# Strassen combinations of h in a stream of their own, in a hybrid decoder block

## The chip, the core and the metric

The kernel runs on one core of one Trainium2 chip. It is one launch, written in Bass with the Tile framework. The metric is the time of the launch on the device in microseconds (us). The five engines are TensorE (PE), VectorE (DVE), ScalarE (ACT), GpSimd (POOL) and SyncE (SP). SP issues every DMA of this kernel. Each engine works through its own instructions in the order in which they were placed when the program was built.

## The reference

For x of shape (1, 2048, 1024) in float32 the layer computes:

```
mod = c @ w_ada + b_ada -> shift/scale/gate for the mixer and for the FFN
h = rms_norm(x, g_pre_mix) * (1 + scale_m) + shift_m
proj = h @ w_in -> attn q (512) k (128) v (128), mLSTM q k v o (512 each), i f (8), gates A B (1024 each)
branch A: rotary q, k; sliding window (128) GQA with sinks, 8 query and 2 key heads of 64
branch B: causal conv4 + SiLU on mLSTM q, k; chunkwise stabilised mLSTM; head norm; sigmoid(o)
x = x + gate_m * rms_norm((sigmoid(gA) * (A @ w_a) + sigmoid(gB) * (B @ w_b)) @ w_out, g_post_mix)
h2 = modulate(rms_norm(x, g_pre_ffn)); ff = (silu(h2 @ w_gate) * (h2 @ w_up)) @ w_down
x = x + gate_f * rms_norm(ff, g_post_ffn)
```

The products are made in near full float32 precision: each operand is split into a rounded part `hi` and the rest `lo`, and a product is three matmuls, hi·hi + hi·lo + lo·hi (`mm3`).

## The kernel before

**Tiling.** The 2048 tokens are four blocks of 512, and two blocks make a superblock (`superblock(sb)`, with blocks `b0` and `b1`). h of a block is kept transposed, features on the 128 partitions, as eight 128x512 tiles, four per half of the features.

**One superblock.** In this order PE does: attention q and k|v of b0 (`q_kv(b0)`), mLSTM v of b0 (`vm(b0)`), then k|v, q and v of b1, and then fourteen pairs of feature tiles (mLSTM q, k, o and the gates) for both blocks at once. The fourteen pairs use Strassen's scheme (`pair_parts`): seven products instead of eight. Its right operands are the quarters of h, named 11, 21, 12 and 22 (half of the features, then block), and four combinations of them, T1 to T4. Then come the outputs of b0 and of b1. The FFN follows after both superblocks.

**How h of the second block is made.** `hprep(b1)` loads x (two tiles of 256 rows), takes the squares on ACT, scales the rows on DVE, and waits. Then `one(k)` makes one feature tile: four PE transposes into a PSUM tile of the pool `mix`, two ACT passes of 128x512 out of it (L518 writes the rounded hi, L520 writes the plain value v), and a DVE subtraction (L521) for lo. For the second block of a superblock the v of all four quarters are kept in the tiles `HR["T1"]` to `HR["T4"]`. After `one(k)` and `one(k + 4)`, four DVE subtractions of 128x512 (L534 to L537) turn the four v tiles of index k into the combinations T1 to T4, in place.

**How T2 and T4 become operands.** `hsums(("T2", "T4"))` issues two DMAs (L545) that copy the combinations from SBUF to SBUF, 1 MB each, into new buffers, and then makes hi on ACT (L551) and lo on DVE (L552), eight times each. It is spawned when the keys of b1 are about to start. `hsums(("T1", "T3"))` follows when v of b1 is done, since its buffers come from quarter 12 of h.

**What sets the order.** The program is written by `run2` and by streams. `run2` goes through the parts of the projections: it issues the next weight load, splits the weights of the parts ahead (L256 and L257 for q, L259 and L260 for the rest: hi on ACT, lo on DVE), and writes the matmuls of a part. Every matmul adds its planned cost to the planner's clock `now`. After every three matmuls `tick()` lets each stream whose due time has come write its next step; a stream yields how long it wants to wait by that clock, in ns. `finish` moves the clock until a stream is done. Streams are `hprep`, `hsums`, the rotary and transposing of q and k (`q_stream`, `k_stream`), the mLSTM gates (`gates`: DVE work on the pre-gates, PE transposes, scans on DVE, two small DMAs, PE transposes again), and two attention streams that each take every second 128-token block. The Tile framework (`schedule_with_timeline_sim=True`) then places each instruction in the queue of its engine: it follows the order written, but takes another instruction where the first is not ready by the time line that it works out. So the queues are fixed when the program is built.

**Attention.** For a 128-token block `attention(n)` loads q, k and v from a DRAM buffer (`at`, two buffers in SBUF), writes 24 score matmuls into four `mix` banks, copies and masks them (ACT L931, DVE L933), takes the maxima (DVE L938 to L941), 8 exponentials on ACT (L946), the sums on DVE (L948, L949), the division on POOL (L950), transposes of the probabilities on PE, and the product with v. The keys come from `k_stream`: rotary on DVE (L757 to L761), a PE transpose, ACT L797 and DVE L798, and DMA stores (L801).

**Pools.** `mix` and `acc` are four PSUM banks each, `tx` nine SBUF tiles (the evacuated q, k, v and the scratch of the rotary), `big` fourteen SBUF tiles of 1 MB (x, h, the combinations), and split weights four tiles.

Of the kernel before, what the change touches and what calls it, by code (L numbers as in the profile page):

```python
# [28 lines left out]
T2 = 1024  # L29
# [6 lines left out]
NEG = -1.0e30  # L36


L_X, L_HT, L_HS = 16000.0, 1400.0, 1500.0
L_ROPE, L_ROPEK, L_QK, L_ATT2 = 5000.0, 2100.0, 1500.0, 3500.0  # L40
L_GATE, L_SCAN = 1800.0, 3000.0
L_SOFT, L_PT, L_PV = 8000.0, 1300.0, 1000.0
# [29 lines left out]
def decoder_block(ctx: ExitStack, tc: tile.TileContext, a: dict, out: bass.AP, dbg=None):  # L72
# [20 lines left out]
    def nm(s):  # L93
        uid[0] += 1
        return f"{s}{uid[0]}"
# [4 lines left out]
    def mix_tile():  # L100
        return ps_mix.tile([P, 512], F32, tag="mix", name=nm("mix"))
# [7 lines left out]
    def big(shape, dtype=F32):  # L109
        t = bpool.tile([P, 2048], dtype, tag="big", name=nm("big"))  # L110
        return t.rearrange("p (k c) -> p k c", k=shape[0])
# [4 lines left out]
    def load_x(src, big, i):  # L116
        xb = big([2, D])
        nc.sync.dma_start(xb, src[i * 256:(i + 1) * 256, :].rearrange("(t p) c -> p t c", p=P))
        return xb
# [86 lines left out]
    def transpose(o, i):  # L206
        now[0] += 110.0
        k = i.shape[0]
        T.transpose(o, i, ident[:k, :k])  # L209

    def spawn(gen, delay=0.0):
        st = [now[0] + delay, gen, False]
        streams.append(st)
        return st
# [15 lines left out]
    def finish(sts):  # L230
        for st in sts:
            while not st[2]:
                now[0] = max(now[0], min(q[0] for q in streams))
                tick()
# [235 lines left out]
    def rsqrt_of_sumsq(ss, n, eps=EPS):  # L470

        ms = small.tile([P, 4], F32, tag="ms", name=nm("ms"), bufs=4)
        V.tensor_scalar(ms[:, :n], ss, 1.0 / D, eps, op0=ALU.mult, op1=ALU.add)  # L473
        r = small.tile([P, 4], F32, tag="rs", name=nm("rs"), bufs=6)
        G.tensor_tensor(r[:, :n], ms[:, :n], nhalf[:, :n], op=ALU.pow)  # L475
        return r
# [3 lines left out]
    def hc_part(name, i):  # L480
        st = HC.setdefault(name, [None, None])
        if st[i] is None:
            st[i] = big([4, TB], F32R)
        return st[i]

    def hprep(b, first=False):

        odd = b % 2
        xs = []
        xbs = x_first if first else [load_x(x_d[b * TB:(b + 1) * TB, :], big, i) for i in range(2)]  # L490
        V_NAMES = ("T3", "T2") if odd else ("T1", "T4")
        for n in V_NAMES:
            HR[n] = big([4, TB])
        vs = [HR[n] for n in V_NAMES]
        for i in range(2):
            xb = xbs[i]
            ss = small.tile([P, 4], F32, tag="ss", name=nm("ss"), bufs=4)
            for t in range(2):
                for hf in range(2):
                    A.activation(vs[i][:, 2 * t + hf, :], xb[:, t, hf * 512:(hf + 1) * 512], AF.Square,  # L500
                                 accum_out=ss[:, 2 * hf + t:2 * hf + t + 1])
            V.tensor_tensor(ss[:, 0:2], ss[:, 0:2], ss[:, 2:4], op=ALU.add)
            r = rsqrt_of_sumsq(ss[:, 0:2], 2)
            for t in range(2):
                if first:
                    A.activation(xb[:, t, :], xb[:, t, :], AF.Copy, scale=r[:, t:t + 1])
                else:
                    V.tensor_scalar(xb[:, t, :], xb[:, t, :], r[:, t:t + 1], None, op0=ALU.mult)
                xs.append(xb[:, t, :])
        yield L_X  # L510

        def one(k):
            name = f"{k // 4 + 1}{odd + 1}"
            hi, lo = (hc_part(name, i)[:, k % 4, :] for i in range(2))
            ps = mix_tile()
            for t in range(NT):
                transpose(ps[:, t * P:(t + 1) * P], xs[t][:, k * P:(k + 1) * P])
            A.activation(hi, ps, AF.Identity, scale=s1[:, k:k + 1], bias=sh1[:, k:k + 1])  # L518
            v = vs[k // 4][:, k % 4, :]
            A.activation(v, ps, AF.Identity, scale=s1[:, k:k + 1], bias=sh1[:, k:k + 1])  # L520
            (G if first else V).tensor_tensor(lo, v, hi.bitcast(F32), op=ALU.subtract)  # L521

        if not odd:
            for k in range(KD):
                one(k)
                yield L_HT
            return
        for k in range(4):
            one(k)
            yield L_HT  # L530
            one(k + 4)
            yield L_HT
            t1, t2, t3, t4 = (HR[n][:, k, :] for n in ("T1", "T2", "T3", "T4"))
            V.tensor_tensor(t1, t3, t1, op=ALU.subtract)  # L534
            V.tensor_tensor(t3, t2, t3, op=ALU.subtract)
            V.tensor_tensor(t2, t2, t1, op=ALU.subtract)
            V.tensor_tensor(t4, t4, t2, op=ALU.subtract)  # L537
            yield L_HT

    def hsums(names):  # L540

        for name in names:
            raw = HR.pop(name)
            lo = hc_part(name, 1)
            nc.sync.dma_start(lo.bitcast(F32), raw)  # L545
        yield L_HD
        for name in names:
            hi, lo = (hc_part(name, i) for i in range(2))
            for k in range(4):
                v = lo[:, k, :].bitcast(F32)  # L550
                A.copy(hi[:, k, :], v)  # L551
                V.tensor_tensor(lo[:, k, :], v, hi[:, k, :].bitcast(F32), op=ALU.subtract)  # L552
                yield L_HS
# [157 lines left out]
    def c_tile(n):  # L711
        C[n] = kvp.tile([P, MH, MD + 1], F32, tag="cst", name=nm("cst"), bufs=3)
        return C[n]

    hp0 = hprep(0, first=True)
    next(hp0)
    tables = {}
# [18 lines left out]
    def superblock(sb):  # L736
# [83 lines left out]
        def q_kv(b):  # L820
            raw_kv = Raw(load_kv)
            return token_group(srcs_rows(w_in, KD, C_Q), KD, 512, lhs_h(b), evac_q(b), pair_heads=True), token_group([(raw_kv, (lambda r, j=j: r[:, j:j + 2, :]), j, 2) for j in range(0, KD, 2)], KD, 264, lhs_h(b), evac_kv(b))
# [388 lines left out]
        def outputs(b):  # L1211
# [41 lines left out]
            def before_out():  # L1253
                if b == 0:
                    finish(R["ada_m"])
                    R_ada.append(spawn(ada_stream([(4, "scale"), (3, "shift"), (5, "gate")], 9000.0)))
                if b == b1 and b + 1 < NBLK:
                    HC.clear()
                    hps[b + 1] = spawn(hprep(b + 1))
                    tables[sb + 1] = rope_tables(sb + 1)  # L1260
                R["gg"] = big([2, D])[:, 0, :]
                nc.sync.dma_start(R["gg"], gg_m_d)
                if b == b0:
                    end_attention(2 * NT)
                    load_y(b1, 0)
                    load_g(b1, 0)
# [11 lines left out]
        def start():  # L1278
            hps[b1] = spawn(hprep(b1), L_HP2)
# [4 lines left out]
        yield lambda: attend(b0)  # L1284
        yield from vm(b0)
        yield lambda: finish([hps[b1]])
        yield lambda: hps.update(t=spawn(hsums(("T2", "T4"))))
        q1, kv1 = (list(z) for z in q_kv(b1))
        yield from kv1
        yield from q1  # L1290
# [32 lines left out]
    hps = {}  # L1323
# [489 lines left out]
    def program():  # L1813
        for i, ch in enumerate(ADA):
            if i == 3:
                yield lambda: tables.update({0: rope_tables(0)})
            yield lambda ch=ch: first_h(*ch)
        items = [it for sb in range(NSB) for it in superblock(sb)]
        last = max(i for i, it in enumerate(items) if isinstance(it, Part))
        yield from items[:last]  # L1820
        yield lambda: next(phase2)
        yield from items[last:]
# [47 lines left out]
```

## Time and profile before

| what | value |
|---|---|
| median of 3 runs | 2710.49 us (2708.99 to 2712.02) |
| the profiled execution, its own time | 2716.59 us |
| its span, first to last instruction | 2714.9 us |
| PE busy | 2639.2 us (97%) |
| DVE busy | 1986.2 us (73%) |
| ACT busy | 1299.8 us (48%) |
| POOL busy | 148.2 us (5%) |
| DMA queue of SP | 509.61 MB, 56.9% of 16 engines |

The profile shows one execution. In its rows a number such as L534 is the line of the kernel. PE is the matmul stream and PEld its weight loads, which overlap it. `<-` after an instruction's name leads from what it writes to what it reads; behind an idle time it names the instruction that ended the wait. In a time line, the first number is the start and the second the duration, both in us; a start of 75.33 is 75.33 us after the first instruction. In a row by line, three numbers with slashes are the shortest, the median and the longest duration in ns.

### The profile page before, as it was taken

The page shows a single profiled execution, that of the slowest core. Times are in us where ns is not written, and L with a number is a line of the kernel's source. Part 1 is how long each engine was busy: PE and PEld are TensorE (multiplying, and loading weights), DVE is VectorE, ACT ScalarE, POOL GpSimd, SP SyncE. Part 2 cuts the span into 40 slices and gives each one's busy share as a digit, 9 for nine tenths or more (in the row PEclk, how much of TensorE's full clock was granted, in tenths as well). Part 3 has the DMA queues.
Part 4 walks back from the last instruction along what each step waited for, and adds up shares of the span by engine and source line. Part 5 has one row for each costly group of instructions (what it writes and reads, how often), then busy time and mean ns, then how long its engine had stood idle before and what let it go on. Part 6 is the DMA issues. An engine that isn't in the chain of part 4 may idle for free.

```text
span 2714.9 us, 35793 instructions
## 1 busy us (share of the span) xinstructions
PE 2639.2 (97%) x12310; PEld 2138.9 (79%) x12310; DVE 1986.2 (73%) x3906; ACT 1299.8 (48%) x2558; POOL 148.2 (5%) x189
## 2 busy tenths in 40 slices
PE   6989999999998999999999999999999999999998
PEld 4867788888885678888887888888877888888886
DVE  7968788778695778876687777776677676766456
ACT  5556544444755564444563443335554333333444
POOL 2010001100101000110000000000000000000000
PEclk8999999999998999999999999999999999999999
DMA  7654355897574544678765564436675232324566
GB/s 249 206 184 157 128 172 179 269 340 248 196 235 147 196 138 138 213 231 291 251 224 198 175 201 152 155 113 213 215 271 188 97 117 86 113 97 144 186 210 217
DMA packets 353639, 511.90 MB, mean 189 GB/s; under 512 B 25120, under 2 KB 213660, under 8 KB 348208
## 3 DMA queue, kind: packets, MB, share of 16 engines
q1 hardware_dynamic: 353456, 509.61, 56.9%
q8 instruction: 97, 1.59, 0.2%
q14 instruction: 86, 0.70, 0.1%
HBM read 357.12 MB, written 144.02 MB: 185 GB/s over the span
## 4 chain that ended last, share of the span: by engine, by line
PE 85%; DVE 7%; DMA 4%; ACT 2%; issue 1%; POOL 0%; SPq 0%; DVEq 0%; ACTq 0%; POOLq 0%
PE acc L204 61%; PE mix L204 22%; PE mix L209 2%; DVE hl L1357 1%; DVE tm L428 1%; DMA raw<-as_d 1%; ACT tm L946 1%; ACT hl L1356 1%; DMA raw<-in_w_in_dram 1%; DMA at_d<-tx 0%; DMA big<-in_x_dram 0%; DVE wlo L260 0%; DMA tx<-in_w_ada_dram 0%; DVE w L1667 0%; DMA at<-at_d 0%
## 5 line engine op out<-in xcount | busy, mean ns | idle before, releaser
L204 PE MATMUL acc<-big,hl 128*128 128x512 f32 x3936 | 940.8, 394 | 4.3 <-ACT tx L827 1.8
L204 PEld LDWEIGHTS acc<-big,hl 128*128 128x128 f32 x3936 | 733.3, 188 | 172.5 <-issue 13.8
L1356 ACT CAST hl<-raw 128x512 fp32r<-128x512 f32 x732 | 440.1, 621 | 493.4 <-PE acc L204 222.2
L1357 DVE TENSOR_TENSOR hl<-raw,hl 128x512 fp32r<-128x512 f32 x732 | 496.3, 694 | 194.8 <-ACT hl L1356 194.0
L204 PE MATMUL acc<-whi,big 128*128 128x512 f32 (+1 forms) x1280 | 379.3, 377 | 10.8 <-ACT big L518 8.4
L204 PEld LDWEIGHTS acc<-whi,big 128*128 128x128 f32 x1280 | 236.2, 192 | 52.4 <-ACT big L518 8.5
L204 PE MATMUL mix<-big,hl 128*128 128x512 f32 x1056 | 263.9, 391 | 1.7 <-ACT hl L1356 1.1
L204 PE MATMUL acc<-wlo,big 128*128 128x512 f32 (+1 forms) x640 | 241.2, 379 | 6.4 <-DVE wlo L260 6.4
L204 PE MATMUL acc<-hl,hl 128*128 128x512 f32 x1008 | 237.4, 393 | 5.1 <-DVE hl L1357 3.4
L204 PEld LDWEIGHTS mix<-big,hl 128*128 128x128 f32 x1056 | 197.9, 188 | 45.9 <-ACT hl L1356 1.9
L204 PEld LDWEIGHTS acc<-hl,hl 128*128 128x128 f32 x1008 | 187.0, 188 | 50.9 <-DVE hl L1357 8.8
L204 PE MATMUL mix<-hl,hl 128*128 128x512 f32 x792 | 182.7, 391 | 1.3 <-DVE hl L1357 0.9
L204 PEld LDWEIGHTS mix<-hl,hl 128*128 128x128 f32 x792 | 147.9, 188 | 35.3 <-DVE hl L1357 3.1
L204 PE MATMUL acc<-big,whi 128*128 128x512 f32 x512 | 157.4, 393 | 0.0
L260 DVE TENSOR_TENSOR wlo<-raw,whi 128x1024 fp32r<-128x1024 f32 (+1 forms) x96 | 109.0, 1137 | 65.5 <-ACT whi L259 59.8
L259 ACT CAST whi<-raw 128x1024 fp32r<-128x1024 f32 (+1 forms) x96 | 94.3, 983 | 123.8 <-PE acc L204 110.4
L204 PEld LDWEIGHTS acc<-wlo,big 128*128 128x128 f32 x640 | 123.7, 193 | 28.3 <-DVE wlo L260 8.6
L475 POOL TENSOR_TENSOR rs<-ms,nhalf 128x1 f32<-128x1 f32 (+1 forms) x56 | 42.6, 772 | 1617.5 <-DVE ms L473 1610.5
L204 PE MATMUL mix<-hcT4h,hl 128*128 128x512 f32 x352 | 117.7, 395 | 0.7 <-ACT hl L1356 0.7
L204 PE MATMUL acc<-hcT2h,hl 128*128 128x512 f32 x352 | 117.6, 394 | 0.0
L204 PEld LDWEIGHTS acc<-big,whi 128*128 128x128 f32 x512 | 95.4, 188 | 19.2
L204 PE MATMUL acc<-big,wlo 128*128 128x512 f32 x256 | 97.7, 393 | 0.0
(330 smaller groups left out, 3491.5 us busy)
## 6 DMA issues: line engine op xcount, KB each, us to landing
raw<-in_w_in_dram SPq DMA_DIRECT2D x48, 1024.0 KB
as_d<-w SPq DMA_DIRECT2D x154, 256.0 KB
raw<-as_d SPq DMA_DIRECT2D x70, 512.0 KB
raw<-in_w_ffn_gate_dram SPq DMA_DIRECT2D x22, 1024.0 KB
raw<-in_w_ffn_up_dram SPq DMA_DIRECT2D x22, 1024.0 KB
raw<-ws_d SPq DMA_DIRECT2D x40, 512.0 KB
y_d<-tm SPq DMA_DIRECT2D x64, 256.0 KB
tx<-in_w_ada_dram SPq DMA_DIRECT2D x64, 256.0 KB
```

The lines of the kernel that those rows point to most:

```text
L204: T.matmul(o, lhsT=lhsT, rhs=rhs, start=start, stop=stop, skip_group_check=resumed)
L209: T.transpose(o, i, ident[:k, :k])
L259: A.copy(hv, src)
L260: V.tensor_tensor(lv, src, hv.bitcast(F32), op=ALU.subtract)
L428: V.scalar_tensor_tensor(acc, raw[:, k, :], c_, acc, op0=ALU.mult, op1=ALU.add)
L475: G.tensor_tensor(r[:, :n], ms[:, :n], nhalf[:, :n], op=ALU.pow)
L946: A.activation(sc[g][:, j, :], sc[g][:, j, :], AF.Exp, bias=nm_[:, hd:hd + 1], accum_out=sums[:, hd:hd + 1])
L1356: A.copy(v(hi), src)
L1357: V.tensor_tensor(v(lo), src, v(hi).bitcast(F32), op=ALU.subtract)
```

## The change

The four subtractions leave `hprep` and become a generator `hcombos`, which goes through the four indices k and writes two subtractions per step, with 1500 ns of the planner's clock after each step. At its end it goes on with `hsums(("T2", "T4"))`. It is spawned where `hsums` was spawned, with a delay of 12000 ns. In `hprep` the yield after the subtractions goes with them, so its `one(k)` follow each other without the 1400 ns that stood there. The sums themselves and the buffers are the same.

```
-L_X, L_HT, L_HS = 16000.0, 1400.0, 1500.0
+L_X, L_HT, L_HS, L_HCB = 16000.0, 1400.0, 1500.0, 12000.0
...
             one(k + 4)
             yield L_HT
+
+    def hcombos():
+        for k in range(4):
             t1, t2, t3, t4 = (HR[n][:, k, :] for n in ("T1", "T2", "T3", "T4"))
             V.tensor_tensor(t1, t3, t1, op=ALU.subtract)
             V.tensor_tensor(t3, t2, t3, op=ALU.subtract)
+            yield L_HS
             V.tensor_tensor(t2, t2, t1, op=ALU.subtract)
             V.tensor_tensor(t4, t4, t2, op=ALU.subtract)
-            yield L_HT
+            yield L_HS
+        yield from hsums(("T2", "T4"))
...
         yield lambda: finish([hps[b1]])
-        yield lambda: hps.update(t=spawn(hsums(("T2", "T4"))))
+        yield lambda: hps.update(t=spawn(hcombos(), L_HCB))
         q1, kv1 = (list(z) for z in q_kv(b1))
         yield from kv1
         yield from q1
```

More of the change, by code (lines that the diff above doesn't have):

```diff
@@ L36 @@
 NEG = -1.0e30
-L_X, L_HT, L_HS = 16000.0, 1400.0, 1500.0
+L_X, L_HT, L_HS, L_HCB = 16000.0, 1400.0, 1500.0, 12000.0
 L_ROPE, L_ROPEK, L_QK, L_ATT2 = 5000.0, 2100.0, 1500.0, 3500.0
@@ L532, in hprep, with hcombos @@
             yield L_HT
+    def hcombos():
+        for k in range(4):
             t1, t2, t3, t4 = (HR[n][:, k, :] for n in ("T1", "T2", "T3", "T4"))
@@ L535, in hprep @@
             V.tensor_tensor(t3, t2, t3, op=ALU.subtract)
+            yield L_HS
             V.tensor_tensor(t2, t2, t1, op=ALU.subtract)
             V.tensor_tensor(t4, t4, t2, op=ALU.subtract)
-            yield L_HT
+            yield L_HS
+        yield from hsums(("T2", "T4"))
     def hsums(names):
@@ L1286, in superblock @@
         yield lambda: finish([hps[b1]])
-        yield lambda: hps.update(t=spawn(hsums(("T2", "T4"))))
+        yield lambda: hps.update(t=spawn(hcombos(), L_HCB))
         q1, kv1 = (list(z) for z in q_kv(b1))
```

## The prediction

> **What bounds the kernel now.** I read the page first, then a table of stretches, then the time lines of PE and DVE inside them. The page says that PE is the bound.
>
> ```profile
> span 2714.9 us, 35793 instructions
> ...
> PE 2639.2 (97%) x12310; PEld 2138.9 (79%) x12310; DVE 1986.2 (73%) x3906; ACT 1299.8 (48%) x2558; POOL 148.2 (5%) x189
> ```
>
> The change adds and removes no instruction, so PE's 2639.2 us of work stay; it can only win or lose idle time of PE. The table of stretches shows how much there is near the change (start and end, length, then busy time and count of PE, PEld, DVE, ACT, POOL, the granted clock, the DMA share and GB/s). The first three rows are superblock 0: the projections of b0, then the keys and most queries of b1, then the second pair of attention blocks. The last three are the same in superblock 1.
>
> ```profile
> 66.00:110.00 44.00, 41.46 (x256) 36.38 (x255) 40.62 (x107) 28.61 (x49) 1.17 (x2) 1.00 0.57 182
> 110.00:161.00 51.00, 48.95 (x284) 38.99 (x283) 37.70 (x116) 29.07 (x78) 4.70 (x4) 0.97 0.62 194
> 161.00:183.00 22.00, 15.14 (x78) 8.10 (x76) 11.91 (x34) 13.75 (x52) 4.68 (x5) 0.84 0.37 116
> 740.00:781.00 41.00, 38.13 (x235) 33.53 (x234) 37.13 (x104) 22.83 (x39) 0.00 (x0) 1.00 0.59 184
> 781.00:838.00 57.00, 54.40 (x304) 43.53 (x304) 43.53 (x127) 31.05 (x83) 4.53 (x4) 0.97 0.67 227
> 838.00:868.00 30.00, 20.58 (x95) 11.12 (x92) 15.03 (x42) 15.81 (x55) 4.67 (x5) 0.72 0.37 116
> ```
>
> Length less PE gives PE's idle time: 2.54, 2.05 and 6.86 us in superblock 0, and 2.87, 2.60 and 9.42 us in superblock 1, 26.3 us in all, which is the most that the change could win. In the stretch of b0 DVE is the full engine: 40.62 of 44 us and 37.13 of 41 us, 92% and 91%. The time line of PE shows what the idle time of b1 hangs on (start, duration, instruction, and in brackets the idle time before it and what ended it).
>
> ```profile
> 117.70 0.59 PE L204 MATMUL acc<-wlo,big 128*128 128x264 f32 x1 [2.05 <-DVE wlo L260]
> ...
> 122.25 0.41 PE L209 MATMUL mix<-ident,tm 68*128 68x68 f32 x4
> 122.59 1.55 PE L204 MATMUL mix<-at 64*128 64x128 f32 x18
> ...
> 167.22 1.70 PE L204 MATMUL mix<-at 64*128 64x256 f32 x24 [2.75 <-DMA at<-at_d]
> ...
> 181.89 0.69 PE L209 MATMUL mix<-ident,tx 128*128 128x128 f32 x2
> ```
>
> The first attention scores start at 122.59, right behind the last transposes of the gates of b0 (122.25). The second pair of blocks waits for its load at 167.22, which needs a buffer of the first pair. The key transposes of b1 come only at 181.89, behind all of that, because the score banks and these transposes share the four `mix` banks. So 122 to 182 is one chain of latencies, attention pair after attention pair, under which PE has the keys and queries of b1 as filler; the filler runs out near 161, and then PE idles 6.86 us. When this chain starts decides when the stretch ends. It starts behind the keys and gates of b0, which are DVE work in the full stretch.
>
> **What the change does, part by part.**
>
> *The sixteen subtractions leave b0.* The view by tile for 60 to 110 us gives the four lines (count, shortest, median and longest ns, first and last start):
>
> ```profile
> L534 DVE TENSOR_TENSOR big<-big,big x4: 681/684/687, 75.3 to 93.6; 128x512 f32<-128x512 f32 x4
> L535 DVE TENSOR_TENSOR big<-big,big x4: 681/684/689, 80.3 to 97.9; 128x512 f32<-128x512 f32 x4
> L536 DVE TENSOR_TENSOR big<-big,big x4: 682/684/687, 84.5 to 101.3; 128x512 f32<-128x512 f32 x4
> L537 DVE TENSOR_TENSOR big<-big,big x4: 683/686/687, 87.9 to 103.1; 128x512 f32<-128x512 f32 x4
> ```
>
> In the time line of DVE such an instruction frees the engine after 0.60 us, as the starts at 77.87 and 78.47 show:
>
> ```profile
> 75.33 0.68 DVE L534 TENSOR_TENSOR big<-big,big 128x512 f32<-128x512 f32 x1
> ...
> 77.87 0.69 DVE L534 TENSOR_TENSOR big<-big,big 128x512 f32<-128x512 f32 x1
> 78.47 0.70 DVE L260 TENSOR_TENSOR wlo<-raw,whi 128x528 fp32r<-128x528 f32 x1
> ```
>
> So 16 x 0.60 = 9.6 us of DVE time go from each b0 stretch to b1. Directly in front of weight splits that PE waits for, this is worth a little. In superblock 0 the split at 78.47 ends a short wait; two subtractions (1.2 us) leave its front, and one subtraction of lo (L521, the same size) moves up because `hprep` loses its pauses: 0.6 us. In superblock 1 the waits and their causes are these:
>
> ```profile
> 744.37 0.68 DVE L536 TENSOR_TENSOR big<-big,big 128x512 f32<-128x512 f32 x1
> 744.97 0.70 DVE L260 TENSOR_TENSOR wlo<-raw,whi 128x528 fp32r<-128x528 f32 x1
> ...
> 748.80 0.69 DVE L537 TENSOR_TENSOR big<-big,big 128x512 f32<-128x512 f32 x1
> 749.40 0.70 DVE L260 TENSOR_TENSOR wlo<-raw,whi 128x528 fp32r<-128x528 f32 x1
> ```
>
> ```profile
> 745.73 0.39 PE L204 MATMUL acc<-wlo,big 128*128 128x264 f32 x1 [0.92 <-DVE wlo L260]
> ...
> 750.16 0.39 PE L204 MATMUL acc<-wlo,big 128*128 128x264 f32 x1 [1.26 <-DVE wlo L260]
> ...
> 773.57 0.50 PE L204 MATMUL acc<-wlo,big 128*128 128x512 f32 x1 [0.69 <-DVE wlo L260]
> ```
>
> One subtraction ahead of each of the first two splits gives 0.60 + 0.60 us, the wait at 773.57 its 0.69 us, together 1.9 us; I take 2.2, since the rotary work between them moves up too, against a cap of 2.87. The b0 part is then 0.6 + 2.2 = 2.8 us. The bounds are 0 (the tighter `one(k)` put two ACT passes where the pause was, and PE waits for ACT instead) and 2.54 + 2.87 = 5.4 us. `hprep` itself issues no later DMA than before; its loads come ahead of the pauses.
>
> *The chain starts earlier.* The first key evacuation of b0 is here:
>
> ```profile
> 83.03 0.38 ACT L806 COPY tx<-acc 128x264 f32<-128x264 f32 x1
> ```
>
> Two of L534 (above) and two of L535 start before it, so 12 subtractions stand between it and the gates and key streams: 12 x 0.60 = 7.2 us of a full engine. The eight lo of T2 and T4 (L552) also leave the stretch between the gates and the first maxima, since they now come behind the subtractions; the row of one of the two half groups there is
>
> ```profile
> 118.98 2.48 DVE L552 TENSOR_TENSOR big<-big,big 128x512 fp32r<-128x512 f32 x4
> ```
>
> or 4.8 us for eight. Against that, up to 16 x 0.60 = 9.6 us of subtractions enter ahead of the first pair's maxima. If all of them do, DVE still has 7.2 + 4.8 - 9.6 = 2.4 us less to do before these maxima; if none, 12.0 us less. The gain per superblock lies between these, capped by the idle time of its last two stretches: 2.05 + 6.86 = 8.9 and 2.60 + 9.42 = 12.0 us. The spawn delay of 12 us of the planner's clock spans about the keys of b1, so most of the sixteen do meet the masks and maxima; I take 3.6 us, near the low end, for both superblocks, 7.2 us together. A value below nothing is the first rival.
>
> *DMAs and queues.* The two SBUF copies of 1 MB were issued at the start of b1 and are now issued some 24 us of planner time later (12 us of delay and eight steps of 1.5 us):
>
> ```profile
> 105.26 1.22 SPq L545 DMA_DIRECT2D big<-big x2
> ```
>
> On SP they pass behind the key stores, the first attention loads, the v stores, the gates' small DMAs and two weight loads; those no longer queue behind 2 MB. At the new place the copies wait on DVE, and a weight load or attention load behind them on SP waits with them. I count both at nothing: weight loads are issued ahead of their use, and that cover is gone if DVE is more than the length of one part (24 matmuls) behind its plan. The eight ACT roundings (L551) move too, to a time when ACT has room (29.07 of 51 us).
>
> *POOL.* The four divisions (L950) of the first pair lie in the stretch that receives the subtractions.
>
> ```profile
> L950 POOL TENSOR_TENSOR tm<-tm,sums x32: 1038/1040/1496, 137.9 to 981.5; 128x512 f32<-128x512 f32 x32
> ```
>
> At most a division has lost 1.496 - 1.040 = 0.46 us, so the rows allow 4 x 0.46 = 1.8 us per superblock; I take nothing, since the subtractions end before the divisions start. [...]
>
> **The sum.** 2.8 + 7.2 = 10.0 us. The profiled execution took 2716.59 us (1.7 us around its span of 2714.9), 0.2% over the median; the gain is idle time and carries over, so it would give 2706.6 in such an execution and 2710.5 - 10.0 = 2700.5 us by the median.
>
> **The rivals.**
>
> *1. The chain gets longer, slower.* The price is the net DVE work that b1 gains, 9.6 - 4.8 = 4.8 us per superblock, put on the first pair's maxima, with no earlier start because the scores stay behind PE's placed order. Then 2 x 4.8 - 2.8 = +6.8, or 2717 us. For it: DVE in the two b1 stretches would go to (37.70 + 9.6) / 51 = 93% and (43.53 + 9.6) / 57 = 93%, as full as b0 is now. Against it: b0's full stretch feeds this chain. It decides as soon as the start of the scores moves by less than the subtractions cost behind it. Chance 0.22.
>
> *2. The copies meet the softmax, slower.* ACT works in order and has waited for these copies:
>
> ```profile
>   ACT big L551: 16.0, 3
> ```
>
> 16.0 us in three waits, 5.3 us each. If that wait falls among the exponentials of the first pair in both superblocks, it costs 2 x 5.3 - 2.8 = +7.9, or 2718 us. Against it: the copies have less company on the DMA engines later. Chance 0.10.
>
> *3. The idle time only changes place.* At 92% DVE share b0 had 5.8 to 7% PE idle, at 74 to 76% b1 had 4 to 4.6%; with the shares exchanged the losses nearly cancel, and the chain, whose order is placed at build time, ends where it did: 2708 to 2712 us, no measurable change. Chance 0.13.
>
> *4. The divisions are held up* by the subtractions each by a whole subtraction of 0.68 us: 8 x 0.68 = 5.4 us, 2706 us; by the largest loss that the row of L950 shows it would be 2704 us. Chance 0.05, since only late subtractions meet them. [...]
>
> **How the numbers follow.** The forecast has the remaining 0.50, with a range of its own from 2687 (all caps: 8.9 + 12.0 + 2.8 = 23.7 us) to 2705. About 0.2%, 5.4 us, is what a measurement of this kernel can tell from no change. Faster is the forecast, 0.50; same is rivals 3 and 4, 0.18; slower is rivals 1 and 2, 0.32. The range for 8 in 10 leaves out the far end of the caps and both slower rivals at once: 2690 to 2721.
>
> **What would show it.** Right: the b0 stretches show DVE well under 90% and no wait of PE for L260 in them; the first scores start several us earlier against the first keys of b1; the idle time before the second pair's scores and transposes shrinks; the subtractions stand between the key work and the maxima. Wrong: the scores start where they did, DVE stands at 93% between the gates and the maxima, and the waits for POOL L950 and DVE L933 grow; or ACT idles before L551 among the exponentials; or SP holds a weight load behind the copies. A changed order of PE elsewhere, from a moved buffer, would make the prediction wrong without any of these.

## The result: the changed kernel is slower by 0.5%

The changed kernel took 2726.36 us (median), the kernel before 2712.01 us beside it: a ratio of 1.0049, with a 95% interval of 1.0036 to 1.0062, or 14 us more. The profiled execution of the changed kernel took 2726.46 us, 0.1 us over its median. The first profile of the kernel before took 2716.59 us, 5 us over its median, so this part compares with a second profile of it that was taken with the experiments (`before_again`, 2710.25 us). Its rows for the stretches of the prediction are these:

```profile
66.00:110.00 44.00, 41.46 (x256) 36.35 (x254) 40.79 (x108) 28.24 (x48) 0.77 (x2) 1.00 0.57 185
740.00:781.00 41.00, 38.33 (x233) 33.55 (x232) 36.52 (x104) 21.05 (x35) 0.00 (x0) 1.00 0.60 183
1420.00:1450.00 30.00, 27.87 (x117) 21.43 (x117) 21.25 (x36) 11.88 (x20) 0.00 (x0) 1.00 0.65 222
```

The same table for the changed kernel (start and end, length, then busy time and count of PE, PEld, DVE, ACT, POOL, the granted clock, the DMA share and GB/s):

```profile
66.00:110.00 44.00, 39.99 (x243) 34.71 (x242) 39.87 (x106) 27.73 (x46) 0.95 (x2) 1.00 0.58 177
110.00:161.00 51.00, 49.14 (x293) 40.11 (x293) 38.10 (x117) 29.85 (x80) 4.39 (x4) 0.97 0.59 189
161.00:183.00 22.00, 13.64 (x75) 9.03 (x73) 10.94 (x32) 13.36 (x48) 4.17 (x4) 0.79 0.44 137
740.00:781.00 41.00, 35.10 (x202) 30.55 (x201) 33.40 (x90) 18.72 (x33) 0.00 (x0) 0.92 0.53 168
781.00:838.00 57.00, 52.38 (x290) 41.43 (x290) 45.88 (x141) 33.47 (x88) 4.59 (x4) 0.97 0.72 233
838.00:868.00 30.00, 26.74 (x130) 16.05 (x129) 13.56 (x34) 16.10 (x52) 4.17 (x4) 0.98 0.43 130
1420.00:1450.00 30.00, 23.69 (x89) 16.93 (x89) 15.96 (x29) 8.11 (x13) 1.74 (x2) 0.94 0.73 271
```

The b0 stretches should have lost PE idle time; they gained it: 44 - 39.99 = 4.0 us instead of 2.5, and 41 - 35.10 = 5.9 us instead of 2.7. A stretch that the prediction did not look at, the start of the FFN near 1440 us, has 6.3 us instead of 2.1. The view by tile says why b0 got no relief (count, shortest, median and longest ns, first and last start; L537 to L541 are the subtractions, now in `hcombos`):

```profile
L537 DVE TENSOR_TENSOR big<-big,big x4: 674/676/677, 75.1 to 89.1; 128x512 f32<-128x512 f32 x4
L538 DVE TENSOR_TENSOR big<-big,big x4: 674/676/677, 79.5 to 96.2; 128x512 f32<-128x512 f32 x4
L540 DVE TENSOR_TENSOR big<-big,big x4: 671/675/682, 84.3 to 99.8; 128x512 f32<-128x512 f32 x4
L541 DVE TENSOR_TENSOR big<-big,big x4: 676/678/680, 93.9 to 102.5; 128x512 f32<-128x512 f32 x4
```

Before they ran from 75.3 to 103.1 us, now from 75.1 to 102.5. **They did not move.** The kernel's program is traced in one order and then placed engine by engine; an instruction that is traced later is placed earlier where the placing expects its engine free and its operands ready. The subtractions need only the transposed h, so they were put back among the transposes. What did change is the rest: `hprep` lost the pause in which the subtractions had stood, so its eight `one(k)` come closer together, and with another order each rotating buffer got other slots. The places of the instructions on DVE, counted from 0 in the order in which the traces show them, tell where the subtractions stayed and how the lo moved together (superblock 0):

```
                        lo of h (one(k), 8 per block)              first subtractions (t1)
before                  154 162 165 169 187 198 199 209            157 163 188 200
changed                 154 162 165 167 171 175 180 191            157 163 172 181
```

Where the waits came from can be read in b0 of superblock 1. The time line of DVE in the changed kernel:

```profile
743.89 0.69 DVE L538 TENSOR_TENSOR big<-big,big 128x512 f32<-128x512 f32 x1
744.49 0.68 DVE L521 TENSOR_TENSOR big<-big,big 128x512 fp32r<-128x512 f32 x1
745.09 0.69 DVE L540 TENSOR_TENSOR big<-big,big 128x512 f32<-128x512 f32 x1
745.70 0.68 DVE L538 TENSOR_TENSOR big<-big,big 128x512 f32<-128x512 f32 x1
...
746.97 0.70 DVE L260 TENSOR_TENSOR wlo<-raw,whi 128x528 fp32r<-128x528 f32 x1
747.59 0.68 DVE L541 TENSOR_TENSOR big<-big,big 128x512 f32<-128x512 f32 x1
...
748.86 0.68 DVE L540 TENSOR_TENSOR big<-big,big 128x512 f32<-128x512 f32 x1
...
752.67 0.70 DVE L260 TENSOR_TENSOR wlo<-raw,whi 128x528 fp32r<-128x528 f32 x1
```

The subtractions and a lo come in a bunch, the rotary work that they hold up follows, and the split of 752.67 comes 5.7 us after the one at 746.97. Before, the subtractions did not stand so close, and the two splits in this place started 4.4 us apart (744.97 and 749.40 in the rows of the prediction). The time line of PE (the idle time before an instruction and what ended it stand in brackets):

```profile
79.03 0.66 PE L209 MATMUL mix<-ident,tx 128*128 128x128 f32 x4 [1.70 <-ACT big L520]
...
753.43 0.39 PE L204 MATMUL acc<-wlo,big 128*128 128x264 f32 x1 [2.53 <-DVE wlo L260]
...
755.14 0.42 PE L204 MATMUL acc<-wlo,big 128*128 128x264 f32 x1
...
758.57 0.28 PE L204 MATMUL acc<-wlo,big 128*128 128x264 f32 x1
...
773.60 0.50 PE L204 MATMUL acc<-whi,big 128*128 128x512 f32 x1 [2.28 <-ACT tx L811]
...
797.52 0.51 PE L204 MATMUL acc<-whi,big 128*128 128x264 f32 x2 [3.29 <-ACT whi L259]
```

In superblock 0 PE waits 1.70 us for ACT's second pass over a transpose of h (L520). Such a wait was there before, but shorter, as the time line of PE in `before_again` shows:

```profile
77.65 0.66 PE L209 MATMUL mix<-ident,tx 128*128 128x128 f32 x4 [0.59 <-ACT big L520]
```

In superblock 1 PE waits 2.53 us for that split. Shortly behind the wait the matmuls take 0.42 us where the same ones take 0.28 us a little later: this wait also cost clock (granted 0.50 from 754.50 to 757.50 us). The stretch from PE's instruction 3480 to its 3720th (740.3 to 782.6 us in `before_again`) takes 49.1 us in the changed kernel and 42.3 before. Of these 6.8 us, 3.2 are idle time (5.84 against 2.67) and 3.7 are longer busy time.

The start of the FFN is a second, separate loss. The time line of PE there, and two rows of ACT and SP's queue:

```profile
1440.24 0.74 PE L204 MATMUL acc<-hcT2h,hl 128*128 128x512 f32 x1 [3.51 <-ACT w L1502]
1440.78 0.63 PE L204 MATMUL acc<-hcT2l,hl 128*128 128x512 f32 x1
...
1444.21 0.40 PE L204 MATMUL acc<-hcT2l,hl 128*128 128x512 f32 x1
```

```profile
1439.60 0.59 ACT L1502 COPY w<-acc 128x512 f32<-128x512 f32 x1 [6.21 <-DMA x<-tm]
```

```profile
1428.78 0.32 SPq L584 DMA_DIRECT2D x<-tm  x1
```

ACT's first copy out of PSUM in the FFN (L1502) waits 6.21 us for a store of the last x1 row out of a `tm` buffer (L584). The FFN's pool lies over the closed `tm` and `tx` pools. In both kernels its first unit gets slot 2 (slots of 2 KB, counted from the start of the `tm` pool); the last x1 row lay in slot 5 before and lies in slot 2 now. The whole piece (PE's instructions 6700 to 7000) takes 78.6 us instead of 73.3: 3.5 us of idle time and 1.8 us of slower matmuls.

To follow all kernels through one program, the table below takes the start of PE's N-th instruction in each trace (all have 12,310) and gives how much longer than in `before_again` each piece took, in us. The first row, the first profile of the same kernel, shows how far two executions differ by themselves: up to 4 us in the attention stretch of superblock 1. Each row is one execution.

```
                        pause  subtractions   b0,sb0  b1,sb0    b0,sb1     b1,sb1     FFN start
PE's instructions                             200-440 440-1400  3480-3720  3720-4700  6700-7000
before, first profile    yes   b0                0.0    +1.6      +0.2       +4.1       +0.1
changed                  no    b0               +1.7    +0.4      +6.8       +0.1       +5.3
e0_no_delay              no    b0               +1.7    +0.2      +5.4       +1.7       +4.7
e1_tight_only            no    b0               +6.8    -9.8      +4.6       -1.4       +3.2
e4_last_row_in_tx        no    b0               +1.7    +0.1      +4.3       -1.1       -0.1
e7_copies_held           no    b0               +1.7    +4.4      +7.1       +7.8        0.0
e8_pause_in_sb1          sb1   b0               +1.8    -0.3      +0.9       -7.9        0.0
e2_stream_with_pause     yes   b0               +1.5    +3.2      +1.3       -9.2       -0.1
e9_pause_copies_held     yes   b0               -0.1    +0.1      +0.8      -10.6        0.0
e3_really_moved          no    b1               -1.4    -0.5      -2.0       -6.5       -0.1
e5_moved_with_pause      yes   b1               -1.3    -2.7      -1.6       -7.2       +0.1
e6_without_subtractions  no    none             -0.7    -9.0      -1.3       -7.1        0.0
e10 (before without)     yes   none             -0.2    -4.7      -1.9       -8.4        0.0
```

### The profile page after: what moved, and what is told of

Its sections match the earlier page's. It is cut to its first block, busy times and chain, and to the rows that moved or that the text cites. A ratio compares the mean times of both kernels' runs of the same rounds, so it can differ in the third digit from the quotient of the medians.

```text
span 2724.7 us, 35779 instructions
## 1 busy us (share of the span) xinstructions
PE 2643.9 (97%) x12310; PEld 2142.1 (79%) x12310; DVE 1985.3 (73%) x3906; ACT 1301.2 (48%) x2558; POOL 147.3 (5%) x189
## 4 chain that ended last, share of the span: by engine, by line
PE 84%; DVE 6%; DMA 5%; ACT 3%; issue 1%; SPq 0%; POOL 0%; DVEq 0%; POOLq 0%; ACTq 0%
PE acc L204 60%; PE mix L204 22%; PE mix L209 2%; DMA at_d<-tx 1%; DVE hl L1362 1%; ACT tm L951 1%; DVE tm L428 1%; ACT hl L1361 1%; DMA raw<-as_d 1%; DMA raw<-in_w_ffn_down_dram 0%; DMA tx<-in_w_ada_dram 0%; DMA x<-tm 0%; DMA big<-in_x_dram 0%; DMA at<-at_d 0%; DVE big L1362 0%
```

## The experiments

Theory A says that the change did not do what its text says: the subtractions stayed, and the loss comes from what was re-placed, the closer `one(k)` in b0 and the slot at the FFN start. Theory B says that the loss comes from the stream itself, its work or its copies beside b1. The kernels that follow were made from the kernel before or from the changed one, each with the edit shown.

**The closer one(k) alone** (from the kernel before):

```
             one(k + 4)
-            yield L_HT
             t1, t2, t3, t4 = ...
```

> Before, with one edit: the pause between one(k + 4) and its four subtractions is taken out; the subtractions stay in hprep, between the transposes. Theory A (the loss comes from what the change re-places: the closer one(k) and a buffer slot): the placed order of DVE has the first subtractions and the los of h at the same places as the changed kernel, and the last x1 row lies in the slot that the first FFN unit gets, so the run should lose like the changed kernel: 3.5 to 5.2 us of PE waiting for ACT L15xx behind the DMA x<-tm at the FFN start, and 2 to 4 us before it; 2718 to 2727 us. Theory B (the loss comes from the stream: subtractions or copies made beside b1): nothing is streamed, so 2709 to 2715 us, no wait at the FFN start.

It took 2720.73 us, a ratio of 1.0037 (1.0023 to 1.0051). The loss is there without any stream. Its profiled execution (2714.70 us) was its shortest, so the sums of its row in the table are low, but the two places show as expected; first the stretch of b0 in superblock 1, with 5.2 us idle, then PE at the FFN start:

```profile
740.00:781.00 41.00, 35.78 (x209) 30.83 (x208) 34.83 (x101) 18.60 (x31) 0.00 (x0) 0.96 0.59 180
```

```profile
1430.58 0.50 PE L204 MATMUL acc<-hcT2h,hl 128*128 128x512 f32 x1 [3.00 <-ACT w L1496]
```

**The stream, with the pause put back** (from the changed kernel):

```
             one(k + 4)
             yield L_HT
+            yield L_HT
```

> The changed kernel, with one edit: the pause behind each pair of one(k) is put back (a second yield L_HT), and the stream stays. Theory A: the placed order of DVE keeps the subtractions and los of h nearly where they were before, and the last x1 rows lie in slots that the first FFN unit does not get: no wait at the FFN start, 2708 to 2717 us. Theory B: the stream is there, so 2720 to 2728 us.

It took 2704.98 us, 0.9982 (0.9973 to 0.9990): faster than the kernel before, and below the range that theory A gave. Theory B falls. The idle time of PE in the stretches of b0 is what it was before the change, 2.5 and 2.4 us:

```profile
66.00:110.00 44.00, 41.45 (x244) 36.53 (x243) 39.80 (x106) 27.25 (x47) 0.66 (x2) 0.96 0.59 183
740.00:781.00 41.00, 38.59 (x236) 33.85 (x235) 37.52 (x102) 24.72 (x43) 0.00 (x0) 1.00 0.63 202
```

The +1.5 us of e2 for b0 of superblock 0 in the table is therefore clock, not idle time: over these 44 us the granted clock is 0.96 in e2 and 1.00 in `before_again`.

**The subtractions really moved** (from the changed kernel; each of the four lines is held behind everything that was traced before it on DVE):

```
-            V.tensor_tensor(t1, t3, t1, op=ALU.subtract)
+            tc.keep_in_program_order(V.tensor_tensor(t1, t3, t1, op=ALU.subtract))
```

> The changed kernel, with the sixteen subtractions of each superblock held in written order on DVE, so that none is placed ahead of work written before it: here they do leave b0 (the first at place 263 of the DVE order instead of 155). It tests the sum that was predicted, which the changed kernel did not test. If b0's relief is worth what the prediction says (2.8 us of waits and 7.2 us of an earlier chain): 2699 to 2705 us, first scores of superblock 0 ahead of 122.0 us. If its first rival holds (the net DVE work goes on the maxima of the first pair, no earlier start): 2715 to 2722 us, with the wait before the second pair's scores and key transposes longer than 6.86 and 9.42 us of idle time in their stretches. By theory A the wait at the FFN start is absent, because the last row lies in other slots.

It took 2701.58 us, 0.9968 (0.9956 to 0.9981), 8.5 us under the kernel before. The prediction had 2700.5 us for a kernel that does this. The subtractions stand in b1, DVE in b0 of superblock 0 falls from 40.79 to 36.45 us, and the first scores start at 108.65 us, 12 us ahead of the 120.66 of `before_again` (last row below):

```profile
L537 DVE TENSOR_TENSOR big<-big,big x4: 674/682/684, 125.8 to 182.6; 128x512 f32<-128x512 f32 x4
```

```profile
66.00:110.00 44.00, 42.38 (x270) 36.78 (x268) 36.45 (x103) 28.68 (x50) 0.97 (x2) 1.00 0.66 204
740.00:781.00 41.00, 39.93 (x252) 35.09 (x252) 36.62 (x107) 22.06 (x39) 0.00 (x0) 1.00 0.69 215
```

```profile
108.65 1.55 PE L204 MATMUL mix<-at 64*128 64x128 f32 x18
```

```profile
120.66 1.55 PE L204 MATMUL mix<-at 64*128 64x128 f32 x18
```

**The last row in another buffer** (from the changed kernel):

```
-            xr = (tm if late and t == NT - 1 else tx)([P, 512])
+            xr = tx([P, 512])
```

> The changed kernel, with one edit: load_rows takes tx for the last token tile of the last block too, instead of tm, so the last x1 stores read slots 11 and 15 instead of 5 and 2, and the first FFN unit (slot 2) waits for no store. Theory A: PE's wait of 3.5 us at the FFN start goes and the matmuls behind it no longer run slow: 5 us less than the changed kernel, 2719 to 2722 us. If the wait is not what holds PE there (it only hides another, such as the load of the FFN weights): 2725 to 2728 us, with an equal idle time of PE at the same place.

It took 2720.04 us, 1.0034 (1.0021 to 1.0046). Against the changed kernel's 1.0049 this is 4 us, and the intervals of the two overlap; the profile is plainer. The wait is gone, the matmuls run at 0.39 us at once, and the piece takes 73.27 us instead of 78.58:

```profile
1433.34 0.39 PE L204 MATMUL acc<-hcT2h,hl 128*128 128x512 f32 x1
1433.57 0.39 PE L204 MATMUL acc<-hcT2l,hl 128*128 128x512 f32 x1
```

So the store in slot 2 held PE there. The wait shows in the three kernels whose last x1 row lies in slot 2 (changed, e0, e1) and in none of the others, whose last rows lie in eight other slots.

**The move with the pause** (the edits of e2 and e3 together):

> The kernel that really moves the subtractions (e3), with the pause behind each pair of one(k) put back. It asks whether the pause is worth something by itself or only because the subtractions stand in b0. If only because of them: b0 has room without them, so this run is as e3 within its spread, 2697 to 2706 us. If the pause has a worth of its own, of the 15 us by which the stream with the pause (2704.98 us) and the changed kernel with its FFN wait removed (2720.04 us) differ: 2686 to 2692 us.

It took 2699.35 us, 0.9951 (0.9939 to 0.9962), the fastest complete kernel of this study, faster than both given ones. Beside e3 the pause is worth 2 us by the medians and 5 us by the ratios, whose intervals overlap; with the subtractions in b0 the ratios of e2 and e4 lie 0.52% apart, 14 us. So most of what the pause is worth, it is worth because the subtractions stand between the transposes.

**No subtractions at all** (from the changed kernel; T1 to T4 keep raw values, so the products of the mixer are others):

```
         for k in range(4):
-            (the four subtractions and two yields)
+        (eight yields, nothing else)
```

> The changed kernel without the sixteen subtractions of each superblock: T1 to T4 keep the raw values of h, so the mixer's Strassen products are not the reference's; everything else is issued as before. It prices what the moved subtractions cost in b1, against e3 (2701.58 us), which does them there. If b1 covers them, as the prediction's likeliest case has it: 2698 to 2705 us. If they go on the path at the net price of the first rival, 4.8 us per superblock, or at their whole 9.6 us: 2692 or 2682 us. The last x1 rows lie in slots 5 and 1, so no wait for a store at the FFN start.

It took 2698.92 us, 0.9951 (0.9940 to 0.9962). The moved subtractions are 2 x 9.6 = 19.2 us of DVE. Against e3, which has the same pauses, they cost 2.7 us by the medians and 4.6 us by the ratios, whose intervals overlap; against e5, 0.4 us and nothing. So b1 covers most of them.

**The pause in superblock 1 alone** (from the changed kernel):

```
             one(k + 4)
             yield L_HT
+            if b == 3:
+                yield L_HT
```

> The changed kernel with the pause put back in superblock 1 alone. The profiles of e2 and e4 put the gain of the pause in superblock 1 (12 us between PE's instructions 3300 and 4500) and none in superblock 0 (2 us the other way), and the last x1 rows lie in slots 8 and 4, so there is no wait at the FFN start. If that place is right: 2702 to 2709 us, as e2. If each superblock has half of it: 2711 to 2714 us. If it is superblock 0: 2718 to 2722 us.

It took 2707.55 us, 0.9986 (0.9977 to 0.9994). The place was right: b0 of superblock 1 falls from +6.8 to +0.9 us in the table while b0 of superblock 0 keeps its +1.8. The rest of its gain, 7.9 us in b1 of superblock 1, is not explained by b0.

**The stream without its delay** (from the changed kernel):

```
-L_HCB = 12000.0
+L_HCB = 0.0
```

> The changed kernel with the delay of the new stream, L_HCB, set from 12000 to 0. If the subtractions are placed by when their operands are ready, the delay does nothing to them: DVE runs them at the same times in b0 (75 to 103 us in superblock 0), the last x1 row lies in slot 2 as in the changed kernel, and the run takes 2720 to 2728 us with a PE wait of 3 to 4 us at the FFN start. If the written place matters, the subtractions start earlier against the keys of b1 and the time moves by over 5 us either way.

It took 2727.37 us, 1.0058 (1.0046 to 1.0070), as the changed kernel, with the same places of the subtractions on DVE. When a stream is spawned does not say when its instructions run.

**The copies held late** (from the changed kernel, then from e2):

```
-            nc.sync.dma_start(lo.bitcast(F32), raw)
+            tc.keep_in_program_order(nc.sync.dma_start(lo.bitcast(F32), raw))
```

> The changed kernel with only the SBUF copies of T2 and T4 (and of T1 and T3) held in written order on their queue, so the copies, the roundings on ACT and the los behind them come late; the subtractions stay where the changed kernel runs them, in b0, close together. The last x1 rows lie in slots 8 and 7: no wait at the FFN start, so 2720 us (as e4) is the mark. If the loss before the FFN comes from ACT waiting for the copies among the keys of b1 (6.7 us in superblock 0, 2.3 and 3.4 us in superblock 1): 2704 to 2711 us. If it comes from the close order in b0 (5 to 6 us idle between 740 and 781 us instead of 2.4): 2715 to 2722 us.

> The stream with the pause (e2, 2704.98 us), with the copies held as in e7. It splits the 5.6 us by which e5 (2699.35 us) beats e2. If they come from the late copies and roundings: 2697 to 2702 us. If they come from the subtractions that leave b0: 2703 to 2708 us.

On the changed kernel it took 2731.34 us, 1.0075 (1.0063 to 1.0088), outside both ranges; with the pause 2703.60 us, 0.9971 (0.9960 to 0.9982), in its second range. The first says that ACT's waits for the copies are not what the changed kernel loses: without them among the keys b0 of superblock 1 is as bad as it was (+7.1 us),

```profile
740.00:781.00 41.00, 34.80 (x200) 30.36 (x199) 34.79 (x91) 20.12 (x35) 0.00 (x0) 0.92 0.55 172
```

and the attention stretches got worse, by 4.4 and 7.8 us. Why the late copies cost that much only where the pause is missing was not settled. By the second the late copies give 0.11% (0.9982 to 0.9971) of the 0.31% by which e5 beats e2; the rest, 0.20% or 5 us, is left to the subtractions that leave b0. The intervals of e9 overlap both others, so this split is rough.

**The kernel before, once more:**

> The kernel before, profiled once more. Its first profile took 2716.59 us where its runs have a median of 2710 to 2712 us. If PE's idle time in the stretch of the second attention pair of superblock 1 (9.4 us in the first profile) is what varies, this profile shows 3 to 6 us less there; the stretches of b0 (2.54 and 2.87 us idle) and the FFN start (no wait for a store) are the same within 0.5 us.

It took 2710.25 us. Between its two profiles the b0 stretches and the FFN start agree to 0.2 us in the table. What varies is the stretch of the second attention pair in superblock 1, but not by its idle time: PE's idle time from 781 to 868 us is 12.0 us in the first profile and 12.7 in the second. That part of the expectation missed.

**The kernel before without the subtractions** (its four lines taken out of `hprep`, nothing else; T1 to T4 keep raw values):

> The kernel before without the sixteen subtractions of each superblock and without the stream: T1 to T4 keep the raw values of h, so the mixer's Strassen products are not the reference's. It asks whether the gain of the kernels that move the subtractions comes from the relief of b0 or from the stream behind it, since the stream with the pause, which leaves them in b0, gained 5 to 7 us too. If from the relief: 2694 to 2702 us, as e5 and e6 (2699.35 and 2698.92 us). If the stream's other order is needed for it: 2704 to 2709 us. The last x1 rows lie in slots 5 and 8: no wait at the FFN start.

It took 2696.88 us, 0.9944 (0.9931 to 0.9958). So taking the 32 subtractions out gains 15.2 us, far more than the waits that stand directly behind them, and moving them (e5) gains 12.8. No stream is needed for the gain. That all of it comes from the relief of b0 is not shown, since taking them out also re-places the rest:

```profile
66.00:110.00 44.00, 41.76 (x258) 36.34 (x256) 39.82 (x107) 32.27 (x56) 0.87 (x2) 1.00 0.71 222
740.00:781.00 41.00, 40.48 (x251) 35.58 (x249) 35.12 (x103) 24.90 (x42) 0.00 (x0) 1.00 0.83 271
```

## Why the prediction was wrong

**What bounds the kernel** was read rightly. PE is the bound, and all but the FFN loss lies in the stretches that were named.

**The step that failed is the first: "the sixteen subtractions leave b0".** They were priced rightly (0.60 us each) but were placed where they had been. The text took the order of the source as the order on the engine. Among the rivals, the case that the change does not do what it says was missing altogether, although the rows were there to ask it: each subtraction's operands are ready in b0, and nothing made it wait.

**The second failure is a bound.** The prediction noted that without the pause two ACT passes would stand where it was, and that PE might wait for ACT, but set the worst case at a gain of 0. It was a loss: 1.7 to 1.8 us in b0 of superblock 0 and 4.3 to 7.1 us in superblock 1, in every kernel of the table with subtractions in b0 and no pause there (e1, in its short execution, lost 6.8 us in superblock 0). In superblock 0 of the changed kernel 1.5 us of this is idle time (4.0 against 2.5). The wait for ACT's L520 came as described, but the larger one was for DVE's split, behind the bunched subtractions. A part that "loses its pauses" should have been priced by what the bunch puts ahead of the next split, with a sign below nothing.

**Not foreseen: the FFN start,** 5.3 us. The prediction's last sentence allowed for a moved buffer but gave it no price and no place, and no chance of its own.

**The sum, where its premise holds.** In e3 and e5, which do move the subtractions, b0 gains 1.4 + 2.0 = 3.4 and 1.3 + 1.6 = 2.9 us; forecast 2.8. The rest of the two superblocks gains 0.5 + 6.5 = 7.0 and 2.7 + 7.2 = 9.9 us; forecast 7.2. The totals by the medians are 8.5 and 12.8 us; forecast 10.0. That they come so close is in part luck. The even split of 3.6 us per superblock was wrong: superblock 0 starts its scores 12 us earlier and keeps 0.5 to 2.7 us of it. And the larger part, that of b1 in superblock 1, does not need the move: e2, e8 and e9 gain 7.9 to 10.6 us there with the subtractions still in b0. What these have in common with the moved kernels, beyond an undisturbed b0, was not isolated, so the mechanism "the chain starts earlier" is shown for the start of the scores, not for the whole of the gain. The far end of the range, "all caps", took 2.8 us for b0, whose own bound was 5.4.

**DMAs and queues**, counted at nothing: in the changed kernel ACT waits 6.7 us in superblock 0 and 2.3 and 3.4 us in superblock 1 for the copies of T2 and T4; in `before_again` only 1.1 us, in superblock 0. The nearest rows tie them to PE's wait of 3.29 us at 797.52, for a weight split that ACT began behind its last wait for a copy. They may cost something there, but e7 shows that removing them does not recover the loss.

**The rivals.** Rival 1, a longer chain by 4.8 us per superblock, is refuted by e3 and e6: e3 gains 8.5 us with the work in b1, and b1 covers that work but for 0 to 4.6 us in all. Rival 2 was near in that ACT did wait for the copies, but among the keys, not among the exponentials, and not because the copies came some 24 us later, as forecast: in superblock 0 they were issued at 100.5 and 114.3 us, before at 105.3. Its 5.3 us was a mean of three unlike waits, 1.2, 5.2 and 9.6 us, of which only the first was for T2 and T4. Rival 3 names the wrong thing: the idle time of b0 did not change place, it grew. Rival 4 was not put to the test, and no run shows its price, a division held up by a whole subtraction of 0.68 us: a division loses at most 0.46 us in the kernel before (1.496 against 1.040), 0.41 us in the changed one (1.447 against 1.042) and 0.54 us in e5 (1.577 against 1.041). In no run does a subtraction run beside a division: the nearest two are 1.1 us apart in e3 and 0.3 us in e5. So the row of the divisions in e3, with 1.489 us at most against 1.496 before, says nothing on it:

```profile
L955 POOL TENSOR_TENSOR tm<-tm,sums x32: 1038/1041/1489, 121.5 to 974.8; 128x512 f32<-128x512 f32 x32
```

The first profile of the kernel before shows, though, a division and the weight splits beside it both longer, and the prediction read only the division's side. A weight split of L257 has a median of 0.684 us; at 139.11 two of them took 2.14 us beside a division that took 1.35 us instead of 1.04:

```profile
L257 DVE TENSOR_TENSOR wlo<-raw,whi x32: 676/684/1532, 21.8 to 820.7; 128x512 fp32r<-128x512 f32 x32
139.11 2.14 DVE L257 TENSOR_TENSOR wlo<-raw,whi 128x512 fp32r<-128x512 f32 x2
139.35 1.35 POOL L950 TENSOR_TENSOR tm<-tm,sums 128x512 f32<-128x512 f32 x1 [0.40 <-DVE sums L949]
```

## What to carry to other kernels

Where a scheduler places the instructions, moving a line in the source moves nothing unless its operands, its engine or an explicit hold make it wait: look first at where the built program puts it, and price the change by what else the edit shifts, such as spacing and buffer slots. A move off a full engine can be worth more than the waits seen directly behind it (8.5 and 12.8 us here, against 5.4 us of idle PE in the two stretches of b0), but part of such a gain can come from what else is placed anew. And where a pool is laid over a closed one, the last store out of the old pool and the first write into the new one should not share a slot: in the changed kernel that wait took 3.51 us, and the piece around it lost 5.3 us.

## What the runs showed of the hardware

Two waits of PE in the changed kernel cost more than their length. The granted clock falls to half behind a wait of 2.53 us (at 753.43) and one of 3.51 us (at 1440.24), for 3.41 us each (start and end, length, busy times, then the granted clock third from the end):

```profile
748.00:750.90 2.90, 2.90 (x24) 2.69 (x23) 2.90 (x8) 0.56 (x1) 0.00 (x0) 1.00 0.00 0
750.90:753.43 2.53, 0.00 (x1) 0.01 (x1) 2.53 (x6) 0.07 (x1) 0.00 (x0) 1.00 0.00 0
...
754.50:756.00 1.50, 1.50 (x8) 1.50 (x8) 1.50 (x5) 0.00 (x0) 0.00 (x0) 0.50 0.00 0
756.00:757.50 1.50, 1.50 (x9) 1.50 (x8) 1.50 (x5) 0.14 (x1) 0.00 (x0) 0.50 0.68 117
757.50:759.00 1.50, 1.50 (x14) 1.50 (x13) 1.50 (x4) 1.14 (x2) 0.00 (x0) 0.95 1.05 403
...
1440.24:1442.00 1.76, 1.76 (x4) 1.44 (x5) 0.67 (x1) 1.75 (x2) 0.00 (x0) 0.52 0.50 200
1442.00:1443.50 1.50, 1.50 (x5) 1.15 (x4) 1.29 (x2) 0.13 (x1) 0.00 (x0) 0.50 0.07 27
```

At the FFN start 3.5 us of idle time became 5.3 us of loss in this way. Ahead of the wait of 2.53 us PE was fully busy for 2.90 us (the first row), and from 754.50 to 757.50 us, at half clock, it was busy throughout. The prediction counted idle time alone, and so did its caps.

Not every such wait halved the clock. In the traces of the changed kernel and of the kernel before (its first profile) the half-clock stretches start whole multiples of 3.41 us apart (in the changed kernel at 754.24, 774.72 and 1440.32 us, 6 and 195 such periods; in the kernel before at 796.96 and 841.33 us, 13 periods), wherever the waits lie. Five kernels have a wait of 2.5 us for the split near 750 us. In the changed kernel, e4 and e7 the matmuls behind it soon take 0.42 us, in e0 and e1 they stay at 0.28 us. Counted in periods of 3.41 us from where the matmuls of each kernel turn slow, an estimate for the e kernels, 2.2 to 2.5 us of the wait fell into one period in the first three, and at most 1.7 and 1.8 us in e0 and e1. These figures give no sharp limit: in e1 a wait of 1.82 us that ends at 766.08 us fell into one period, and the matmuls behind it take 0.63 us instead of 0.39. At the FFN start a wait of 3.0 us halved the clock in e0 (0.94 granted from 1420 to 1450 us) and one of 3.0 us did not in e1 (1.00; 1.8 us of the wait in one period). So 1.7 us of loss, an estimate from 3.41 us at half clock, hangs on where a wait falls, and by the author's estimate this is part of the scatter in the table.
